# Weight parts of later mixers, made during the feed-forward before and kept in DRAM

## The chip, the core and the metric

The kernel runs on one core of one Trainium2 chip, in one launch. The metric is the device time of the launch in microseconds; the number shown for a kernel is the median of its runs. TensorE (PE) multiplies, VectorE (DVE), ScalarE (ACT) and GpSimd (POOL) do the element-wise work, and SyncE (SP) issues nearly all DMAs. All arithmetic that counts here is in float32.

## The reference

Four layers run one after another on one sequence of 512 tokens with 1024 channels: two layers of a first kind, then two of a second. Each layer is a mixer and a feed-forward:

```
first kind                                     second kind
h = rms_norm(x);  z = h @ w_in      (2560)     h = rms_norm(x);  p = h @ w_in_2    (10032)
attention, HGRN2 both ways, convolution        NSA, stick-breaking, GLA, forgetting attention
x = x + concat(mixers) @ w_out                 x = x + (sum of gate_n * (y_n @ w_branch_n)) @ w_out_2
x = x + square(relu(rms_norm(x) @ w1)) @ w2    x = x + square(relu(rms_norm(x) @ w1)) @ w2
```

The feed-forward is 1024 to 4096 to 1024 in all four layers.

## The kernel before

**Products of split operands.** A float32 product is made of three matmuls on a rounded type. Each operand is split into a high part (a rounded copy, by ACT) and a low part (the operand minus the high part, by DVE); `mm3` adds high·high, low·high and high·low in one PSUM bank. The activations (`xh`, `xl`) are split once a layer. A weight is split where it is used: `wload` (L321) takes a weight in units of 128 partitions x 512 floats (256 KB), loads each into a tile `wr` by a DMA on SP (L330), copies it to `wh` and writes the rest to `wl`. There are 4 `wr`, 4 `wh` and 3 `wl` tiles. A unit is four 128x128 blocks and 12 matmuls of 512 columns, or, in `nlater`, two blocks of 256 columns and 24 matmuls of 256 columns.

**Who splits.** `split` (L312) uses ACT (L315) and DVE (L316). In the mixers of the first kind, a counter (`share`, `pool_share`) lets the first 8 units go that way, and all later ones give the subtraction to POOL instead (L334 ACT, L335 POOL):

```
self.share += self.pool_share
if self.share >= 1.0:
    self.share -= 1.0
    nc.scalar.activation(hi, raw, AF.Copy)
    nc.gpsimd.tensor_tensor(lo, raw, hi.bitcast(F32), op=ALU.subtract)
else:
    self.split(hi, lo, raw)
```

**The order of the work.** Mixers are Python generators that `weave` runs by written-out times; projections that a mixer needs later are `Later` objects in a queue, and each step of a mixer advances the queue by a set rate (`pace`, `step`). Nothing of it is decided on the chip: the program is one fixed list of instructions for each engine, with semaphores between them, and a scheduler that the program asks for puts that list together. In a layer of the first kind the two HGRN heads, the convolution and the attention are woven, and then the attention's rest with half of the output projection. In the second kind NSA comes first, with its own projections (`nsa_inputs`, `compress`) and those of the queue beside it, then stick-breaking, GLA and the forgetting attention. `compress` loads other weights as they are into the same four `wr` tiles (L1477) and multiplies them unsplit (L1482).

**The feed-forward.** `mlp` (L496) goes in four chunks of 1024 hidden channels: 8 products with `w1` (ACT relu, POOL square, split into `hid`), then 8 products with `w2` (DVE times `R2`, POOL adds to `x`). That makes 64 products of two units each. In the last chunk `post(m)` makes the next layer's `xh`, `xl` and sums of squares.

Of the kernel before, what the change touches and what calls it, by code (L numbers as in the profile page):

```python
# [19 lines left out]
F32 = mybir.dt.float32  # L20
F32R = mybir.dt.float32r
# [8 lines left out]
T = 512  # L30
D = 1024
KT = D // 128
# [129 lines left out]
class Core:  # L162
    def __init__(self, ctx, tc, const):
        self.tc, self.nc = tc, tc.nc
        nc = self.nc
# [21 lines left out]
        self.keep = tc.dram_tile([KT, 128, T], F32, name="keep")  # L187
        self.pad(self.core_w, 96)
# [132 lines left out]

    def wload(self, pieces, a, b):

        nc = self.nc
        out, n = [], 512 // b
        for i in range(0, a, n):
            m = min(n, a - i)
            raw, hi, lo = self.wtile("wr", m, b), self.wtile("wh", m, b, F32R), self.wtile("wl", m, b, F32R)
            for ap, rows, cols in pieces:
                nc.sync.dma_start(raw[rows, :, cols], ap[:, i:i + m])  # L330
            self.share += self.pool_share
            if self.share >= 1.0:
                self.share -= 1.0
# [4 lines that stand above are left out]
            out += [(hi[:, k], lo[:, k]) for k in range(m)]  # L338
        return out

    def wcols(self, w, k0=0, kt=KT):

        v = w[k0 * 128:(k0 + kt) * 128, :].rearrange("(k p) c -> p k c", p=128)
        return self.wload([(v, slice(None), slice(None))], kt, v.shape[2])
# [155 lines left out]
    def mlp(self, w1, w2, post, tags, fc=1024):  # L500

        nc = self.nc
        nfc, nk = w1.shape[1] // fc, fc // 128
        R2 = self.t(tags["r2"], "R2")
        for c in range(nfc):
            hs = []
            for m in range(nk):
                col = c * fc + m * 128
                pz = self.tproj(w1[:, col:col + 128])
                r, s = self.t(tags["r"], "r"), self.t(tags["s"], "s")  # L510
                nc.scalar.activation(r, pz, AF.Relu)  # L511
                nc.gpsimd.tensor_tensor(s, r, r, op=ALU.mult)  # L512
                a, b = (self.t(tag, "hid", F32R) for tag in tags["h"][m])
                self.split(a, b, s)
                hs.append((a, b))
                if c == 0 and m == 1:
                    nc.vector.tensor_tensor(R2, self.R, self.R, op=ALU.mult)
            for m in range(KT):
# [4 lines left out]
                (nc.vector if last and m == KT - 1 else nc.gpsimd).tensor_tensor(self.x[m], self.x[m], s, op=ALU.add)  # L523
                if last:
                    post(m)

# [294 lines left out]
class First:  # L821
# [219 lines left out]

    def hgrn(self, l, pr, vi, slot, mix):
# [6 lines left out]
        for half in range(2):  # L1049
            h = 2 * pr + half  # L1050
            wv = lambda c: w[:, c:c + 64].rearrange("(k p) c -> p k c", p=128)
            ws = K.wload([(wv(1280 + h * 64), slice(None), slice(0, 64)),
                              (wv(1536 + h * 64), slice(None), slice(64, 128))], KT, 128)
# [194 lines left out]
    def layer(self, l, gmlp, post):  # L1248
# [17 lines left out]
        K.out_proj(w[0:512], [K.parts(y, "h", "hx") for y in at], lambda m: K.prep(m, gmlp()))  # L1266
        K.mlp(I["w_mlp_in"][l], I["w_mlp_out"][l], post,
# [12 lines left out]
class Second:  # L1280
# [120 lines left out]


    def narrow(self, l, other):
        K, nc, I = self.K, self.K.nc, self.I
        w = I["w_in_2"][l]
        ws = K.wload([(w[:, c:c + 32].rearrange("(k p) c -> p k c", p=128), slice(None), slice(32 * i, 32 * i + 32))
                          for i, c in enumerate((O_NG, O_FF, O_GA, O_GA))], KT, 128)
# [609 lines left out]
    def layer(self, l, gff, post):  # L2017
# [31 lines left out]
                   lambda m: K.prep(m, gff()), kept=True)  # L2049
        K.mlp(I["w_ff1_2"][l], I["w_ff2_2"][l], post,  # L2050
# [60 lines left out]
```

## Time and profile before

| | us |
|---|---|
| median of three runs | 3739.27 |
| lowest and highest run | 3739.17, 3741.41 |
| the profiled execution | 3740.83 |
| its span (first to last instruction) | 3738.3 |
| mean granted clock of TensorE | 0.989 |

The profile is of one execution, so what is summed from it is summed against 3740.83. Of the span, the feed-forwards take 347 to 697, 1012 to 1382, 2178 to 2528 and 3370 to the end (the second and the last with a piece of what stands around them); the mixers lie between, the first from 0. "Busy" of PE needs care: a 512-column matmul is drawn as some 390 ns, but in a feed-forward 1550 matmuls fill 350 us, one each 226 ns, so short waits of PE hide under the drawn ends.

### The profile page before, as it was taken

The numbers are of one execution on the slowest core, as the hardware profiler recorded it, in microseconds if no ns is written. First come the engines' busy times: TensorE is split into PE (matmuls) and PEld (weight loads), VectorE is DVE, ScalarE is ACT, GpSimd is POOL, SyncE is SP. The second block draws the span as 40 slices with busy tenths as digits, with TensorE's granted clock in tenths as the row PEclk, the third lists the DMA queues.
The fourth block names the chain that finished last, engine by engine and source line by source line (L and its number), as shares of the span: only waits on it lengthen the run. The fifth ranks groups of instructions, "written<-read, shape, count | busy, mean of one in ns | idle before, by whom it ended". The sixth has DMA issues, their size and how long they took to land.

```text
span 3738.3 us, 53178 instructions
## 1 busy us (share of the span) xinstructions
PE 3620.1 (97%) x18793; PEld 3010.6 (81%) x18793; DVE 2316.7 (62%) x4554; ACT 1900.7 (51%) x3940; POOL 947.6 (25%) x925
## 2 busy tenths in 40 slices
PE   8889999987999999999999999999999999999999
PEld 7757888885788887888788888887888888788887
DVE  8885333699543346787778753335687777874334
ACT  6575333467643343678554643334567744553333
POOL 4732222466122230001213122222001121222222
PEclk9999999999999999999999999999999999999999
DMA  4102333321133344213222243334312223233332
GB/s 130 52 12 77 96 98 96 113 60 29 43 96 96 98 117 128 55 46 75 65 72 68 74 114 97 97 98 128 93 32 71 71 65 77 60 105 95 97 97 87
DMA packets 561851, 306.65 MB, mean 82 GB/s; under 512 B 49978, under 2 KB 551344, under 8 KB 561584
## 3 DMA queue, kind: packets, MB, share of 16 engines
q1 hardware_dynamic: 558128, 296.95, 28.8%
q10 hardware_dynamic: 3456, 6.29, 0.4%
q8 instruction: 148, 2.42, 0.3%
q14 instruction: 119, 0.97, 0.1%
HBM read 292.68 MB, written 10.49 MB: 81 GB/s over the span
## 4 chain that ended last, share of the span: by engine, by line
PE 84%; DVE 11%; ACT 2%; issue 1%; DMA 1%; POOL 1%; SPq 0%; POOLq 0%; DVEq 0%; ACTq 0%
PE pm L348 21%; PE pm L350 21%; PE pm L349 21%; PE po L645 2%; PE pm L395 2%; PE pm L394 2%; PE pm L396 2%; DVE cy L1207 1%; PE pt L627 1%; PE pa L1022 1%; DVE X L1114 1%; DVE X L1115 1%; DVE acc L1136 1%; DVE nm L592 1%; PE pt L1959 1%
## 5 line engine op out<-in xcount | busy, mean ns | idle before, releaser
L316 DVE TENSOR_TENSOR wl<-wr,wh 128x512 fp32r<-128x512 f32 x956 | 677.9, 709 | 753.3 <-issue 383.2
L315 ACT ACTIVATE wh<-wr 128x512 fp32r<-128x512 f32 x956 | 600.8, 629 | 1039.8 <-PE pm L349 899.7
L348 PE MATMUL pm<-xh,wh 128*128 128x512 f32 x2160 | 855.0, 396 | 6.8 <-DVE zq L1048 2.8
L350 PE MATMUL pm<-xh,wl 128*128 128x512 f32 x2160 | 850.4, 394 | 7.8 <-POOL wl L335 7.8
L349 PE MATMUL pm<-xl,wh 128*128 128x512 f32 x2160 | 846.9, 393 | 0.0
L350 PEld LDWEIGHTS pm<-xh,wl 128*128 128x128 f32 x2160 | 407.1, 188 | 94.7 <-POOL wl L335 10.9
L348 PEld LDWEIGHTS pm<-xh,wh 128*128 128x128 f32 x2160 | 407.5, 189 | 89.4 <-DVE z L560 3.5
L349 PEld LDWEIGHTS pm<-xl,wh 128*128 128x128 f32 x2160 | 407.6, 189 | 82.6 <-issue 2.8
L350 PE MATMUL pm<-hid,wl 128*128 128x512 f32 x1024 | 398.1, 389 | 0.0
L349 PE MATMUL pm<-hid,wh 128*128 128x512 f32 x1024 | 398.0, 389 | 0.0
L348 PE MATMUL pm<-hid,wh 128*128 128x512 f32 x1024 | 396.5, 389 | 0.0
L523 POOL TENSOR_TENSOR x<-x,os 128x512 f32<-128x512 f32 x124 | 206.2, 1663 | 421.8 <-DVE os L521 420.1
L512 POOL TENSOR_TENSOR s<-r 128x512 f32<-128x512 f32 x128 | 135.0, 1055 | 572.2 <-ACT r L511 533.1
L394 PE MATMUL pm<-wh,xh 128*128 128x256 f32 x896 | 257.8, 291 | 5.5 <-ACT wh L315 3.9
L395 PE MATMUL pm<-wl,xh 128*128 128x256 f32 x896 | 258.0, 289 | 2.3 <-DVE wl L316 2.1
L396 PE MATMUL pm<-wh,xl 128*128 128x256 f32 x896 | 256.3, 287 | 0.0
L349 PEld LDWEIGHTS pm<-hid,wh 128*128 128x128 f32 x1024 | 192.2, 188 | 40.1
L350 PEld LDWEIGHTS pm<-hid,wl 128*128 128x128 f32 x1024 | 192.2, 188 | 39.9
L348 PEld LDWEIGHTS pm<-hid,wh 128*128 128x128 f32 x1024 | 192.2, 188 | 39.7
L348 PE MATMUL pm<-mxh,wh 128*128 128x512 f32 x512 | 202.3, 398 | 8.3 <-ACT mxh L315 5.3
L521 DVE TENSOR_TENSOR os<-pm,R 128x512 f32<-128x512 f32 x128 | 88.5, 692 | 191.5 <-PE pm L350 191.5
L349 PE MATMUL pm<-mxl,wh 128*128 128x512 f32 x512 | 202.8, 396 | 0.9 <-DVE mxl L316 0.9
(619 smaller groups left out, 6753.3 us busy)
## 6 DMA issues: line engine op xcount, KB each, us to landing
wr<-in_w_in_dram SPq DMA_DIRECT2D x376, 256.0 KB
wr<-in_w_ff_dram SPq DMA_DIRECT2D x256, 256.0 KB
wr<-in_w_mlp_in_dram SPq DMA_DIRECT2D x128, 256.0 KB
wr<-in_w_mlp_out_dram SPq DMA_DIRECT2D x128, 256.0 KB
wr<-in_w_out_dram SPq DMA_DIRECT2D x64, 256.0 KB
wr<-in_w_branch_dram SPq DMA_DIRECT2D x64, 256.0 KB
xo<-keep SPq DMA_DIRECT2D x32, 256.0 KB
keep<-x ACTq DMA_DIRECT2D x24, 256.0 KB
```

What stands on the lines that cost most here:

```text
L315: nc.scalar.activation(hi, src, AF.Copy)
L316: nc.vector.tensor_tensor(lo, src, (hi if hi_in is None else hi_in).bitcast(F32), op=ALU.subtract)
L348: nc.tensor.matmul(out, wh, xh, start=start, stop=False)
L349: nc.tensor.matmul(out, wh, xl, start=False, stop=False)
L350: nc.tensor.matmul(out, wl, xh, start=False, stop=stop)
L394: nc.tensor.matmul(o, self.xh[kk][:, c], h, start=f, stop=False, skip_group_check=True)
L395: nc.tensor.matmul(o, self.xh[kk][:, c], l, start=False, stop=False, skip_group_check=True)
L396: nc.tensor.matmul(o, self.xl[kk][:, c], h, start=False, stop=e, skip_group_check=True)
L512: nc.gpsimd.tensor_tensor(s, r, r, op=ALU.mult)
L521: nc.vector.tensor_tensor(s, po, R2, op=ALU.mult)
L523: (nc.vector if last and m == KT - 1 else nc.gpsimd).tensor_tensor(self.x[m], self.x[m], s, op=ALU.add)
L645: nc.tensor.matmul(*x, start=start and n == 0, stop=stop and n == len(mm) - 1, skip_group_check=True)
```

## The change

During each of the first three feed-forwards the kernel also splits weights of the mixer that follows. `split_ahead` makes a list of jobs, one for each unit: a load of the unit into a tile (`c` in the first kind, `g` in the second) on SP's queue; at the next step ACT's copy and DVE's subtraction into two more tiles; at the step after that two stores of 256 KB, issued on ACT's queue, into a DRAM tile. `background` is called after each of the 64 products and starts jobs at an even rate. `wload` asks for each unit whether it was kept; if so, it loads both parts straight into `wh` and `wl` by two DMAs on SP and neither takes a `wr` tile nor splits, and the counter of `pool_share` isn't moved.

Kept are 48 units for layer two (all of `w_in`, and rows 512 to 1024 of `w_out`), and 62 units each for layers three and four (the first gate's eight column blocks, the narrow columns, NSA's keys, values and queries, and stick-breaking's inputs). Layer one, GLA, the forgetting attention, the branches and the rest of the output projections load and split as before.

```diff
+    def units(self, pieces, a, b):
+        n = 512 // b
+        return [([(ap[:, i:i + min(n, a - i)], rows, cols) for ap, rows, cols in pieces], min(n, a - i))
+                for i in range(0, a, n)]
...
+    def split_ahead(self, tags, wanted, steps):
+        nc, todo = self.nc, [(u, m, b) for w in wanted for u, m in self.units(*w) for b in (w[2],)]
+        def job(unit, m, b):
+            view = lambda t: t[:, :m * b].rearrange("p (a b) -> p a b", a=m)
+            raw = view(self.t(tags[0], "pr"))
+            for ap, rows, cols in unit:
+                nc.sync.dma_start(raw[rows, :, cols], ap)
+            yield
+            hi, lo = (self.t(tag, "pp", F32R) for tag in tags[1:])
+            self.split(view(hi), view(lo), raw)
+            yield
+            d = self.tc.dram_tile([2, 128, T], F32, name="parts")
+            for i, x in enumerate((hi, lo)):
+                nc.scalar.dma_start(d[i][:, :m * b], x[:, :m * b].bitcast(F32))
+            self.kept[self.unit_key(unit)] = d
+        self.jobs, self.running = [job(*t) for t in todo], []
+        self.job_rate, self.job_credit = len(todo) / steps, 0.0
+
+    def background(self, last=False):
+        if not self.jobs and not getattr(self, "running", None):
+            return
+        self.job_credit += self.job_rate
+        while self.running or (self.jobs and last):
+            self.running = [j for j in self.running if next(j, self) is not self]
+            if not last:
+                break
+        while self.jobs and self.job_credit >= 0.5:
+            self.job_credit -= 1
+            j = self.jobs.pop(0)
+            next(j)
+            self.running.append(j)
...
     def wload(self, pieces, a, b):
-        out, n = [], 512 // b
-        for i in range(0, a, n):
-            m = min(n, a - i)
-            raw, hi, lo = self.wtile("wr", m, b), self.wtile("wh", m, b, F32R), self.wtile("wl", m, b, F32R)
-            for ap, rows, cols in pieces:
-                nc.sync.dma_start(raw[rows, :, cols], ap[:, i:i + m])
+        out = []
+        for unit, m in self.units(pieces, a, b):
+            hi, lo = self.wtile("wh", m, b, F32R), self.wtile("wl", m, b, F32R)
+            d = self.kept.pop(self.unit_key(unit), None)
+            if d is not None:
+                for i, x in enumerate((hi, lo)):
+                    nc.sync.dma_start(x.bitcast(F32), d[i][:, :m * b].rearrange("p (a b) -> p a b", a=m))
+                out += [(hi[:, k], lo[:, k]) for k in range(m)]
+                continue
+            raw = self.wtile("wr", m, b)
+            for ap, rows, cols in unit:
+                nc.sync.dma_start(raw[rows, :, cols], ap)
             self.share += self.pool_share
...
     def mlp(self, w1, w2, post, tags, fc=1024):
                 self.split(a, b, s)
                 hs.append((a, b))
+                self.background()
...
                 (nc.vector if last and m == KT - 1 else nc.gpsimd).tensor_tensor(self.x[m], self.x[m], s, op=ALU.add)
+                self.background()
                 if last:
                     post(m)
+        self.background(last=True)
...
     First.layer
+        nxt = self.ahead(1) if l == 0 else Second.ahead(K, I, 0)
+        K.split_ahead(("c", "hz", "hx"), nxt, 64)
         K.mlp(I["w_mlp_in"][l], I["w_mlp_out"][l], post,
...
     Second.layer
+        K.split_ahead(("g", "z", "k"), self.ahead(K, I, 1) if l == 0 else [], 64)
         K.mlp(I["w_ff1_2"][l], I["w_ff2_2"][l], post,
```

`First.ahead` and `Second.ahead` list the units in about the order in which the mixers take them; `both_ways` and `narrow_columns` give two loads that gather columns a name, so that both places ask for the same unit.

## Rows read from the trace of the kernel before

**Rows 1.** The page, part 1: busy time, share of span, instructions by engine.

```profile
...
PE 3620.1 (97%) x18793; PEld 3010.6 (81%) x18793; DVE 2316.7 (62%) x4554; ACT 1900.7 (51%) x3940; POOL 947.6 (25%) x925
...
```

**Rows 2.** Windows by stage: us, PE, PEld, DVE, ACT, POOL, clock, DMA, GB/s.

```profile
...
697.00:1012.00 315.00, 280.20 (x1571) 222.12 (x1570) 251.43 (x417) 202.69 (x415) 159.87 (x162) 0.96 0.17 48
1382.00:2178.00 796.00, 781.59 (x4527) 664.21 (x4526) 609.44 (x1445) 473.98 (x1090) 122.46 (x154) 1.00 0.29 76
2178.00:2528.00 350.00, 350.00 (x1551) 289.66 (x1550) 139.38 (x208) 123.83 (x211) 85.82 (x68) 1.00 0.35 102
...
```

**Rows 3.** Windows inside mixers two, three and four; columns as in rows 2.

```profile
...
760.00:935.00 175.00, 148.58 (x863) 120.47 (x862) 162.20 (x257) 115.02 (x234) 116.11 (x113) 0.94 0.14 40
1390.00:1490.00 100.00, 93.67 (x558) 76.46 (x557) 68.32 (x259) 37.50 (x78) 7.73 (x26) 0.98 0.47 131
1490.00:1650.00 160.00, 158.61 (x1132) 140.52 (x1131) 129.11 (x383) 109.87 (x320) 2.44 (x4) 1.00 0.18 46
2550.00:2650.00 100.00, 94.29 (x568) 76.89 (x568) 53.25 (x146) 38.55 (x79) 8.24 (x20) 1.00 0.44 121
...
```

**Rows 4.** Chain of waits by line: 760:935, 1390:1490, 2550:2650.

```profile
...
by line: DVE cy L1207 13.8%; DVE acc L1136 5.3%; DVE X L1114 5.2%; DVE X L796 5.1%; DVE X L806 4.8%; issue 4.3%; DVE X L1115 4.2%; DVE X L795 4.1%; DVE nm L592 3.9%; PE ps L1126 3.9%; DVE rot L934 2.9%; DVE qs L669 2.4%; PE pm L394 2.0%; PE
...
by line: DVE cb L1463 8.3%; PE pm L395 8.1%; PE pm L394 7.8%; PE pm L396 7.5%; DMA wr<-in_w_in_dram 6.0%; DMA wr<-in_nsa_cmp_wv_dram 5.3%; DVE wl L316 5.1%; PE pm L348 5.1%; PE pm L350 5.0%; PE pm L349 5.0%; SPq L217 4.9%; PE ps L1482 4.6%;
...
by line: PE pm L348 14.2%; PE pm L350 13.8%; PE pm L349 13.7%; DMA wr<-in_nsa_cmp_wv_dram 8.7%; PE pm L395 7.2%; PE pm L394 6.7%; PE pm L396 6.5%; SPq L1477 6.3%; DMA wr<-in_w_in_dram 5.7%; PE ps L1482 4.8%; DVE wl L316 2.0%; issue 1.5%; AC
...
```

**Rows 5.** Groups by form, VectorE, 697:1012: busy us, mean ns | idle before.

```profile
...
L1207 DVE SCALAR_TENSOR_TENSOR cy<-u,cw,cy 128x512 f32<-128x512 f32 x30 | 33.7, 1124 | 0.3
...
L1114 DVE TENSOR_TENSOR X<-X,x 128x256 f32<-128x256 f32 x18 | 13.7, 763 | 0.7 <-ACT X L807 0.7
L796 DVE TENSOR_TENSOR X<-z,m 128x256 f32<-128x256 f32 x12 | 11.1, 925 | 0.0
...
L316 DVE TENSOR_TENSOR wl<-wr,wh 128x512 fp32r<-128x512 f32 x9 | 6.2, 690 | 8.4 <-issue 6.4 <-PE pm L350 1.2 <-ACT xh L445 0.9
...
```

**Rows 6.** Lines 1207, 1114, 796 in 697:1012: duration ns minimum/median/maximum.

```profile
...
L1207 DVE SCALAR_TENSOR_TENSOR cy<-u,cw,cy x30: 731/878/1848, 792.7 to 908.5; 128x512 f32<-128x512 f32 x30
...
L1114 DVE TENSOR_TENSOR X<-X,x x18: 408/425/1516, 749.9 to 956.7; 128x256 f32<-128x256 f32 x18
...
L796 DVE TENSOR_TENSOR X<-z,m x12: 411/726/1539, 731.1 to 930.4; 128x256 f32<-128x256 f32 x12
...
```

**Rows 7.** Timeline from 915: start us, us, engine, line, operation.

```profile
...
915.08 1.46 POOL L1205 TENSOR_TENSOR cy<-cy,tap 128x512 f32<-128x512 f32 x1 [0.90 <-ACT tap L1204]
...
915.32 1.49 DVE L796 TENSOR_TENSOR X<-z,m 128x256 f32<-128x256 f32 x1
...
917.67 0.41 DVE L796 TENSOR_TENSOR X<-x 128x256 f32<-128x256 f32 x1
...
```

**Rows 8.** Groups by form of GpSimd, 697 to 1012; columns as in rows 5.

```profile
...
L335 POOL TENSOR_TENSOR wl<-wr,wh 128x512 fp32r<-128x512 f32 x39 | 57.2, 1470 | 28.9 <-PE pm L396 10.5 <-PE pm L350 7.1 <-ACT wh L334 4.3
...
```

**Rows 9.** Pieces of the chain, 1390 to 1490: start us, us, what.

```profile
...
1452.51 3.06 DMA wr<-in_w_in_dram
1455.59 0.64 ACT wh L315
1456.26 0.69 DVE wl L316
...
```

**Rows 10.** DMA issues on SyncE's and ScalarE's queues: duration ns minimum/median/maximum.

```profile
...
L330 SPq DMA_DIRECT2D wr<-in_w_mlp_in_dram x16: 367/368/368, 428.2 to 468.4; - x16
...
L1477 SPq DMA_DIRECT2D wr<-in_nsa_cmp_wk_dram x16: 595/601/622, 1420.1 to 1464.4; - x16
...
L450 ACTq DMA_DIRECT2D keep<-x x5: 326/326/327, 1360.2 to 1378.3; - x5
...
```

**Rows 11.** Groups by form of TensorE, 1390 to 1490; columns as in rows 5.

```profile
...
L394 PE MATMUL pm<-wh,xh 128*128 128x256 f32 x96 | 27.4, 295 | 2.2 <-ACT wh L315 2.2
L348 PE MATMUL pm<-xh,wh 128*128 128x512 f32 x54 | 21.6, 401 | 1.4 <-DVE z L560 1.4
...
```

More of the change, by code (lines that the diff above doesn't have):

```diff
@@ L187, in __init__ @@
         self.keep = tc.dram_tile([KT, 128, T], F32, name="keep")
+        self.kept, self.jobs = {}, []
         self.pad(self.core_w, 96)
@@ L320, in wtile, with unit_key @@
         return self.core_w.tile([128, n], dt, name=tag, tag=tag, bufs=WEIGHTS[tag])[:, :a * b].rearrange("p (a b) -> p a b", a=a)
+    def units(self, pieces, a, b):
+        n = 512 // b
+        return [([(ap[:, i:i + min(n, a - i)], rows, cols) for ap, rows, cols in pieces], min(n, a - i))
+                for i in range(0, a, n)]
+    @staticmethod
+    def unit_key(unit):
+        return tuple((ap.tensor.name, ap.offset, str(ap.ap), str(cols)) for ap, rows, cols in unit)
+    def split_ahead(self, tags, wanted, steps):
[15 more added lines that the diff above has]
+        self.job_rate, self.job_credit = len(todo) / steps, 0.0
@@ L339, in wload, with wrows, wanted @@
         return out
+    @staticmethod
+    def wrows(w, k0=0, kt=KT):
+        v = w[k0 * 128:(k0 + kt) * 128, :].rearrange("(k p) c -> p k c", p=128)
+        return [(v, slice(None), slice(None))], kt, v.shape[2]
     def wcols(self, w, k0=0, kt=KT):
-        v = w[k0 * 128:(k0 + kt) * 128, :].rearrange("(k p) c -> p k c", p=128)
-        return self.wload([(v, slice(None), slice(None))], kt, v.shape[2])
+        return self.wload(*self.wrows(w, k0, kt))
+    def wanted(self, w, *cols):
+        out = []
+        for c, n in cols:
+            per = 512 // n
+            out += [self.wrows(w[:, c:c + n], i, per) for i in range(0, w.shape[0] // 128, per)]
+        return out
     def mm3(self, out, wh, wl, xh, xl, start, stop):
@@ L1039, in att_out, with both_ways, ahead @@
         return y
+    @staticmethod
+    def both_ways(w, h):
+        wv = lambda c: w[:, c:c + 64].rearrange("(k p) c -> p k c", p=128)
+        return [(wv(1280 + h * 64), slice(None), slice(0, 64)), (wv(1536 + h * 64), slice(None), slice(64, 128))], KT, 128
+    def ahead(self, l):
+        K, w, o = self.K, self.I["w_in"][l], self.I["w_out"][l]
+        out = K.wanted(w, (768, 128)) + [self.both_ways(w, 0)] + K.wanted(w, (896, 128)) + [self.both_ways(w, 2)]
+        out += K.wanted(w, (2304, 128), (512, 256), (2048, 128), (1024, 256)) + [self.both_ways(w, 1), self.both_ways(w, 3)]
+        out += K.wanted(w, (2432, 128), (0, 256), (2176, 128), (256, 256), (1792, 128), (1920, 128))
+        return out + K.wanted(o[512:1024], *((m * 128, 128) for m in range(KT)))
     def hgrn(self, l, pr, vi, slot, mix):
@@ L1050, in hgrn @@
             h = 2 * pr + half
-            wv = lambda c: w[:, c:c + 64].rearrange("(k p) c -> p k c", p=128)
-            ws = K.wload([(wv(1280 + h * 64), slice(None), slice(0, 64)),
-                              (wv(1536 + h * 64), slice(None), slice(64, 128))], KT, 128)
+            ws = K.wload(*self.both_ways(w, h))
             pz = K.pt()
@@ L1400, in rope, with ahead, narrow_columns @@
         nc.vector.tensor_tensor(v[:, :, 0:16], v[:, :, 0:16], b, op=ALU.add)
+    @staticmethod
+    def ahead(K, I, l):
+        w = I["w_in_2"][l]
+        out = K.wanted(w, (O_GATE, 128)) + [Second.narrow_columns(w)]
+        out += K.wanted(w, (O_KC, 128), (O_VC, 128), (O_KS, 256), (O_KS + 256, 256), (O_Q, 256), (O_Q + 256, 256))
+        out += K.wanted(w, *((O_GATE + m * 128, 128) for m in range(1, KT)))
+        out += K.wanted(w, (O_SB + 1024, 256), (O_SB, 128), (O_SB + 512, 128), (O_SB + 128, 128), (O_SB + 640, 128))
+        return out + K.wanted(w, (O_SB + 1280, 256), *((O_SB + c, 128) for c in (256, 768, 384, 896)))
+    @staticmethod
+    def narrow_columns(w):
+        return [(w[:, c:c + 32].rearrange("(k p) c -> p k c", p=128), slice(None), slice(32 * i, 32 * i + 32))
+                for i, c in enumerate((O_NG, O_FF, O_GA, O_GA))], KT, 128
     def narrow(self, l, other):
@@ L1405, in narrow @@
         w = I["w_in_2"][l]
-        ws = K.wload([(w[:, c:c + 32].rearrange("(k p) c -> p k c", p=128), slice(None), slice(32 * i, 32 * i + 32))
-                          for i, c in enumerate((O_NG, O_FF, O_GA, O_GA))], KT, 128)
+        ws = K.wload(*self.narrow_columns(w))
         p = K.pt()
```

## The prediction

> **What bounds the kernel now.** I read the page first. PE is drawn busy 97% of the span, the other engines far less [rows 1], so a gain must come out of PE's waits, and only 118 us of idle time is drawn. Then the windows by stage. The feed-forwards have none of it: 350.00 of 350.00 us, and DVE and ACT are at 139 and 124 us there. Layer two's mixer is the loose one: PE has 280.2 of 315 us, 34.8 idle, at a granted clock of 0.96; layer three's has 14.4 idle in 796 us [rows 2]. Inside layer two, from 760 to 935, PE idles 26.4 of 175 us while DVE is busy 162.2 [rows 3], and the chain of waits runs through DVE lines (1207, 1136, 1114, 796, 806), hardly through products of weights [rows 4]. DVE sets the pace of that stretch.
>
> Layers three and four are loose at their start, where NSA's projections run: 6.3 and 5.7 us of PE are idle in 100 [rows 3]. There the chain does go through weights. In a window of 100 us a percent is a microsecond: 6.0 us of raw loads and 5.1 us of subtractions `wl` in layer three, 5.7 and 2.0 in layer four [rows 4]. One round of it: a load of 3.06 us, then ACT's copy of 0.64, then DVE's 0.69 [rows 9]; the four `wr` tiles are shared with `compress`, so the load starts late. After that, in 1490 to 1650, PE is idle 1.4 us [rows 3].
>
> **The change, part by part.**
>
> *Layer two.* All 40 units of `w_in` and 8 of `w_out` come as parts. Two things leave DVE's stretch. First, the eight subtractions that DVE makes itself, 8 x 0.69 = 5.5 us [rows 5]. Second, GpSimd's: 57.2 of its 159.9 busy us [rows 8, 2]. These count because GpSimd's work slows DVE's. An L796 of 128x256 that starts 0.24 us after a GpSimd instruction of 1.46 us takes 1.49 us; two microseconds later, with GpSimd still, one takes 0.41 [rows 7]. Over the stage three groups show it best, by their mean against their minimum [rows 5, 6]: L1207 30 x (1.124 - 0.731) = 11.8 us, L1114 18 x (0.763 - 0.408) = 6.4, L796 12 x (0.925 - 0.411) = 6.2, together 24.4. The weight subtraction is 57.2/159.9 = 0.36 of GpSimd's time, so 8.7 us of that is its own: the floor, for these groups are only 58.5 of DVE's 251.4 busy us. The ceiling is that each of them holds DVE for its whole length, 57.2, but no more than PE's idle 34.8 can come out. I take twice the floor, 18, since the one pair shown is a nearly full hold and other DVE groups lose too. With 5.5 it is 23.5 us of DVE; before 760 and after 935 DVE isn't always last, so I count 22, with ends of 8 and 34.8. ACT's 48 copies go too, but ACT has 202.7 of 315 us and isn't what is waited for.
>
> The Trainium skill bears on the pair (SBUF — State Buffer, section "Who interferes with whom"): VectorE and GpSimd share one pair of ports as an exclusive lock, and a VectorE instruction with two SBUF inputs waits for the whole of a GpSimd instruction that reads SBUF. By that rule alone the sum takes the ceiling in place of 18; the trace agrees for the pair, 1.49 against 0.41 us, and only in part for the sum, where the median L1114 is at its minimum. The rival "all of it" is what this rule gives.
>
> *Layers three and four, the dense start.* A kept unit needs no `wr` tile, no copy and no subtraction. Of layer three's chain 5.1 us of `wl` and some 3 of `wh` (pieces of 0.64) are gone. Of the 6.0 of raw loads none, some or all come back as waits for the parts: the trace shows no load into `wh` or `wl`. Its cost is bounded by nothing (landed before PE asks) and by its landing. Two issues of 0.37 us [rows 10] and a landing as in rows 9 make 3.4 to 3.8 us from the moment a tile is free. It may be filled once PE has left the unit three before, so two units of PE's work cover it: a unit takes 12 x 0.226 = 2.7 us, from 1550 matmuls in 350 us [rows 2], so 5.4 us. That covers it by the nearest row, so I count 9 us in layer three, ends 0 and 14. In layer four 2.0 of `wl`, about as much of `wh`, and a part of 5.7: 6, ends 0 and 9.
>
> *The rest of NSA and stick-breaking.* 62 subtractions are 43 us of DVE's 609 in a mixer [rows 2]. From 1490 DVE has 129 of 160 us but PE hardly idles, so little is to be had: 3 us a layer for what hides under PE's drawn ends, ends 0 and 8.
>
> *The feed-forwards.* A job adds 0.64 + 2 x 0.33 = 1.3 us to ACT (the stores' issues are on its queue [rows 10]) and 0.69 to DVE. For 62 jobs that is 80 and 43 us on top of 124 and 139, in 350 [rows 2]: both stay under 60%. On SP it is 62 x 0.37 = 23 us among loads that are four `wr` tiles ahead. In bytes it is 62 x 0.77 MB = 48 MB in 350 us, 137 GB/s on top of 102. At the stage's own price (0.35 for 102) the DMA share would go to 0.82; the highest share of the rows shown is 0.47 [rows 3], so this is the part that I know least. What covers it is that every load is wanted several units later. The stores' wait for DVE's subtraction stands on ACT's queue a whole product (5.4 us) after it, with the next relu and weight copies behind it. I count nothing in the loop, and at each of three ends a copy and a subtraction that stand ahead of the last `post(m)`, 1.3 at most: 2 us in all. If the cover fails, 172 jobs pay.
>
> *SP's queue.* The part loads stand in line with all else on it. In layer three the constants' issues take 4.9 us of the chain [rows 4], and a kept unit behind them has only 5.4 us of cover where a raw unit had four `wr` tiles and three `wl`: 2 us, ends 0 and 5.
>
> The sum: -22 - 9 - 6 - 6 + 2 + 2 = -39 us, so 3740.8 - 39 = 3701.8 for the profiled execution. The median of the runs is 1.6 us below that execution, so **3700**.
>
> **The rivals.**
>
> *All of it.* GpSimd's hold costs DVE its full length and PE's whole idle time of layer two goes (34.8), the weights' chain in layers three and four too (14 and 9), 6 for the rest, less 4: -60, 3679. For it: DVE at 93% in the stretch, and the full hold in rows 7. Against: with DVE shorter, the HGRN levels' own chain through PE and ACT stands there. Chance 0.15.
>
> *Little of it.* What GpSimd still does (102.7 us, its convolution adds above all) closes up and holds DVE instead, so layer two gives its 5.5 and a little, 8; the loads of parts take the place of the raw loads, 8 and 3; with 2 and 4: 3741 - 8 - 8 - 3 - 2 + 4 = 3724, so 3722. For it: line 1205's adds are as long as the subtractions (1.46 against 1.47 us, rows 7, 8). Chance 0.17.
>
> *Given back.* The jobs delay the feed-forwards' own splits or loads. At 0.2 us for each of 172 jobs that is 34 us, 3734 for the runs; or the names of the units don't match and the mixers load and split as before, 3743. Against the first: PE doesn't wait once in 350 us. Chance 0.07.
>
> *Slower: three buffers are too few.* The load of a `wl` tile waits for PE, with SP's later loads behind it. If parts land later than 5.4 us after release, PE waits in each dense unit. In the 100 us of layer three there are 96/8 + 54/4 = 25.5 such units [rows 11], in both layers 51. At 6.7 us it is 1.3 x 51 = 66 us; the gains there are gone and layer two's 22 stay: 3741 - 22 + 66 + 4 = 3789, so 3787. From about 5.8 us on, layer two's gain is eaten. For it: `compress` puts four issues of 0.6 us [rows 10] between the parts, 2.4 us, and two loads take the place of one. Against: 3.4 to 3.8 us without them. Chance 0.11.
>
> The Trainium skill (DMA: Bandwidth & Descriptors, section "Latency and other measured facts") speaks for this rival: access to HBM is 0.2 us on average and 2 us at high load. With 1.8 us more, an estimate from that page, the parts would land 5.2 to 5.6 us after release, at the edge of the cover. No run here shows such a load yet; at a share of 0.47 the landing is 3.06 us.
>
> **How the numbers follow.** The forecast holds 0.50, with a range of its own from 3687 to 3714, by the ends of layer two's term. Faster by over 0.2% (7.5 us, about what can be told here) takes the forecast and the first two rivals, 0.80 of their 0.82; slower takes 0.12; the rest, 0.08, is the same. From 3672 to 3735 the forecast, both other faster cases and half of "given back" lie; outside are the slower case and the tails, some 0.19.
>
> **What would show it.** In the profile after: no L335 left in layer two's mixer, L1207's and L1114's means there near their minima, DVE's busy time lower by about 23 us and the stage shorter by about as much. In 1390 to 1490 no `wr` of `w_in`, no `wl` on DVE; if PE now waits for DMA into `wh` or `wl`, the slow rival has begun. The three feed-forwards at the same length within 1 us, DMA share 0.6 to 0.8. I would be wrong if a feed-forward grows by over 3 us, if layer two's mixer gains under 8 us, or if waits for the parts sum to over 20 us.

## The result, and the profile after

The changed kernel takes 3774.39 us (median of 4 runs, 3769.68 to 3776.63); the kernel before, on the same chip, 3740.34 (4 runs). The ratio is 1.0087, with an interval from 1.0074 to 1.0099. The change makes the kernel 34 us slower, where 39 us faster was forecast. The profiled execution of after took 3772.6 us, its span 3770.8.

Where did the time go? Both kernels have the same 18793 matmuls, so their progress can be compared: when PE starts its n-th matmul in each. This table is worked out from the two traces. The first column is a time in the span of before, the others say how many microseconds later (+) or earlier the changed kernel stands at the same count, and how much of that came since the mark above. Inside a mixer the scheduler puts some matmuls in another order, so there the n-th is not always the same one; the marks are read to a tenth or two.

```
mark in before        what lies above the mark              after stands    since the mark above
 697                  mixer one, feed-forward one           +13.7           +13.7
1012                  layer two's mixer                      -2.4           -16.1
1382                  feed-forward two                      +17.7           +20.1
1490                  layer three's dense start             +10.2            -7.5
2080                  rest of layer three's mixer           +17.9            +7.7
2528                  its output, feed-forward three        +41.8           +23.9
2650                  layer four's dense start              +36.4            -5.5
end                   rest of layer four                    +33.0            -3.4
```

The mixers do give time back, 16.1 us in layer two and 7.5 and 5.5 at the two dense starts. The feed-forwards, at which the prediction counted 2 us in all, take 57.7.

Of before, the windows over feed-forwards one and two (as in [rows 2]: us, then PE, PEld, DVE, ACT, POOL, clock, DMA share, GB/s); the third is in [rows 2]:

```profile
347.00:697.00 350.00, 350.00 (x1550) 289.63 (x1549) 137.78 (x210) 125.62 (x215) 93.75 (x69) 1.00 0.35 102
1012.00:1382.00 370.00, 370.00 (x1640) 306.22 (x1639) 150.49 (x230) 135.35 (x229) 97.39 (x72) 1.00 0.35 101
```

And of after: the same three feed-forwards, then layer two's mixer and layer three's dense start:

```profile
348.00:711.00 363.00, 355.97 (x1552) 289.67 (x1551) 179.06 (x256) 147.79 (x255) 94.88 (x71) 1.00 0.60 189
1010.00:1400.00 390.00, 377.78 (x1640) 306.15 (x1639) 206.39 (x291) 166.54 (x287) 95.80 (x72) 0.99 0.68 216
2199.00:2570.00 371.00, 359.32 (x1554) 290.49 (x1553) 186.75 (x264) 154.39 (x265) 87.13 (x69) 0.99 0.64 205
...
711.00:1010.00 299.00, 276.90 (x1571) 219.56 (x1570) 215.20 (x409) 179.67 (x371) 104.17 (x123) 0.97 0.32 99
...
1407.70:1500.20 92.50, 90.05 (x558) 74.12 (x557) 52.06 (x234) 21.52 (x51) 6.87 (x26) 1.00 0.70 212
```

1640 matmuls that filled 370 us take 390, and PE idles 12.2 of them. Yet DVE has only 206 of the 390 us, ACT 167, the DMA engines 0.68: no engine is near its end. That speaks against the amount of work and for the place where it stands; the experiments below test it. The page's 40 slices (94 us each; DMA busy tenths, then GB/s) show how unevenly it stands:

```profile
DMA  4106933541498346323232399335622223233332
GB/s 130 51 12 205 338 118 96 159 130 42 123 338 295 95 133 203 107 79 76 65 74 62 83 347 341 104 97 168 186 68 82 73 62 76 66 100 99 98 98 87
```

The traffic that the prediction had evenly at 0.82 over a feed-forward is at 0.8 to 0.9 and 295 to 347 GB/s in its first half (slices 5, 12 and 13, 24 and 25), and falls back to 95 to 118, about what before has, in the slice after (6, 14, 26). The instructions of the jobs' part tiles say the same (number, duration in ns minimum/median/maximum, first and last start in us):

```profile
L349 ACTq DMA_DIRECT2D parts<-pp x344: 325/327/1852, 302.1 to 2356.4; - x172
L316 ACT ACTIVATE pp<-pr x172: 610/624/645, 300.6 to 2346.5; 128x512 fp32r<-128x512 f32 x172
L317 DVE TENSOR_TENSOR pp<-pr,pp x172: 675/685/1802, 324.6 to 2355.6; 128x512 fp32r<-128x512 f32 x172
its engine sat idle before it (us, times) until:
  DMA pr<-in_w_in_dram: 49.0, 30
  ACT pp L316: 36.1, 33
  DVE pp L317: 23.3, 18
  DMA parts<-pp: 19.4, 9
```

The first copy is at 300.6 us, in mixer one, 47 us before the feed-forward in whose loop it is written, and the last of layer four's at 2346.5, where that feed-forward goes on to 2570. The scheduler has put the jobs into the engines' lists far ahead of where `background` stands in the program; that it goes as early as their tiles allow is my reading. And in an engine's list nothing overtakes: while ACT waits for a job's load (49.0 us in all), everything behind stands still. One such place in feed-forward two, from the timeline of after (start, duration, engine; in brackets the idle time before, and what ended it):

```profile
1052.25 0.63 ACT L316 ACTIVATE pp<-pr 128x512 fp32r<-128x512 f32 x1 [0.82 <-DMA pr<-in_w_in_dram]
1052.29 2.77 SPq L342 DMA_DIRECT2D pr<-in_w_in_dram  x3
1052.31 4.16 ACTq L349 DMA_DIRECT2D parts<-pp  x3
...
1056.57 0.63 ACT L316 ACTIVATE wh<-wr 128x512 fp32r<-128x512 f32 x1 [3.69 <-DMA parts<-pp]
...
1057.23 1.49 DVE L317 TENSOR_TENSOR wl<-wr,wh 128x512 fp32r<-128x512 f32 x2 [3.03 <-ACT wh L316]
...
1058.86 0.60 ACT L577 ACTIVATE r<-pm 128x512 f32<-128x512 f32 x1 [0.87 <-DVE wl L317]
...
1059.51 0.79 PE L414 MATMUL pm<-xh,wh 128*128 128x512 f32 x1 [4.29 <-ACT r L577]
```

Three stores hold ACT's queue for 4.16 us. The third is issued only at 1056.14: its queue waits for a semaphore whose last update comes at 1056.07, from the landing of a store issued at 1050.49. Behind the stores stands a weight's copy, behind it DVE's `wl`, then the relu that empties the PSUM bank, and PE stands 4.29 us, its longest wait in that feed-forward. It is a wait for an eviction that has nothing to do with any job.

### The profile page after: what moved, and what is told of

It reads as the page before. It is cut to its first block, busy times and chain, and to the rows that moved or that the text cites. A ratio compares the mean times of both kernels' runs of the same rounds, so it can differ in the third digit from the quotient of the medians.

```text
span 3770.8 us, 54180 instructions
## 1 busy us (share of the span) xinstructions
PE 3629.7 (96%) x18793; PEld 2999.2 (80%) x18793; DVE 2352.8 (62%) x4594; ACT 1895.0 (50%) x3940; POOL 888.7 (24%) x885
## 4 chain that ended last, share of the span: by engine, by line
PE 76%; DVE 6%; DMA 6%; ACT 2%; issue 1%; POOL 0%; ACTq 0%; SPq 0%; DVEq 0%; POOLq 0%
PE pm L414 19%; PE pm L416 19%; PE pm L415 19%; PE pm L460 2%; PE pm L461 2%; PE pm L462 2%; DMA pr<-in_w_in_dram 2%; DMA parts<-pp 2%; PE po L714 2%; PE pt L696 1%; DVE pp L317 1%; DVE wl L317 1%; DMA wr<-in_w_mlp_out_dram 1%; DVE nm L661 1%; PE pa L1091 1%
## 5 line engine op out<-in xcount | busy, mean ns | idle before, releaser
L317 DVE TENSOR_TENSOR wl<-wr,wh 128x512 fp32r<-128x512 f32 x824 | 605.2, 736 | 577.5 <-issue 266.9
L316 ACT ACTIVATE wh<-wr 128x512 fp32r<-128x512 f32 x824 | 515.3, 628 | 759.0 <-PE pm L415 648.9
L416 PEld LDWEIGHTS pm<-hid,wl 128*128 128x128 f32 x1024 | 192.2, 188 | 52.0 <-DVE wl L317 12.5
L416 PE MATMUL pm<-mxh,wl 128*128 128x512 f32 x512 | 203.2, 397 | 0.7 <-DVE wl L317 0.7
```

Of the source, the lines that this page charges most:

```text
L316: nc.scalar.activation(hi, src, AF.Copy)
L317: nc.vector.tensor_tensor(lo, src, (hi if hi_in is None else hi_in).bitcast(F32), op=ALU.subtract)
L416: nc.tensor.matmul(out, wl, xh, start=False, stop=stop)
```

## The experiments

All were compared with the kernel before on the same chips; its medians there were 3741.05, 3739.96 and 3740.77 us for the three groups of runs below.

**First group: which part of a job costs?**

*e1_paced.* Each job's load keeps its place in SP's list:

```
-                nc.sync.dma_start(raw[rows, :, cols], ap)
+                self.tc.keep_in_program_order(nc.sync.dma_start(raw[rows, :, cols], ap))
```

> The changed kernel, and each job's load is pinned behind the SyncE load that stands before it in the program, so that jobs run at the written rate (one in 1.0 to 1.3 products) instead of in the first 150 us of a feed-forward. Crowding theory (it doesn't matter whether through DMA or through the engines' lists): the 58 us that the three feed-forwards and the projections before them lost fall under 10, DMA share there under 0.75, time 3715 to 3730. Amount theory (172 jobs cost what they cost, wherever they stand): the loss stays above 40, time 3758 to 3775.

Measured: 3753.5 us, ratio 1.0036 [1.0023, 1.0048], so 21 us better than the changed kernel, and in neither of the two ranges. By the progress of PE feed-forward one now costs 1.0 us in place of 13.7, all of it ahead of the loop; the other two still cost 19.8 and 20.4. That is not spread either: between marks 12 us apart it comes in four steps of 3.7 to 5.8 us in each of the two, one at the turn from the first to the second half of each chunk, and almost nothing in between. The first of them, from the timeline:

```profile
1080.07 0.63 ACT L316 ACTIVATE pp<-pr 128x512 fp32r<-128x512 f32 x1 [2.64 <-DMA pr<-in_w_in_dram]
...
1080.73 0.69 DVE L317 TENSOR_TENSOR pp<-pr,pp 128x512 fp32r<-128x512 f32 x1 [3.03 <-ACT pp L316]
...
1081.94 0.68 DVE L588 TENSOR_TENSOR os<-pm,R 128x512 f32<-128x512 f32 x1
...
1082.77 0.47 PE L414 MATMUL pm<-hid,wh 128*128 128x512 f32 x1 [1.82 <-DVE os L588]
```

ACT waits 2.64 us for a job's load, DVE 3.03 for ACT's copy, and the eviction `os` stands behind both until PE has no free bank.

*e2_no_split.* Jobs load and store, but don't split; the raw tile is stored twice, so the parts are not the weight's parts and the products come out otherwise:

```
...
-            self.split(view(hi), view(lo), raw)
...
-                nc.scalar.dma_start(d[i][:, :m * b], x[:, :m * b].bitcast(F32))
+                nc.scalar.dma_start(d[i][:, :m * b], raw.rearrange("p a b -> p (a b)"))
```

> The changed kernel without the jobs' copy and subtraction: the raw unit is loaded and stored twice, so DMA traffic of the jobs is whole and ACT and DVE have only the two store issues a job; the mixers' products use wrong parts. DMA theory (loads of the feed-forward's own weights land late among the jobs' bytes): loss in the feed-forwards stays at 45 or more of 58, time 3760 to 3780. Lists theory (copies and subtractions that wait for their loads stand ahead of the feed-forward's own on ACT and DVE): loss under 15, time 3720 to 3735.

*e3_no_traffic.* The first job of a layer runs whole; all others split one resident tile of ones and neither load nor store, and all kept units load the first one's parts (the same remark on the products):

```
+            if first:
+                self.kept[self.unit_key(unit)] = first["d"]
+                yield
+                raw = first["raw"]
+                hi, lo = (self.t(tag, "pp", F32R) for tag in tags[1:])
+                self.split(hi, lo, raw)
+                yield
+                return
...
```

> The changed kernel with only one unit a layer loaded and stored; every further job makes its copy and its subtraction from a tile that lies there, with no load and no store, and all kept units in the mixers load that one pair of parts (products wrong). DMA theory: the feed-forwards lose under 10 of 58, time 3715 to 3728. Lists theory: they lose 40 or more, time 3755 to 3770.

*e4_one_job.* One whole job a layer, the others do nothing; the mixers load as many parts as in the changed kernel (the first job's). It is the mixers' side alone:

```
+            if first:
+                self.kept[self.unit_key(unit)] = first["d"]
+                return
...
```

> The mixers' side alone: one job a layer, and every kept unit loads that one pair of parts (products wrong). All theories: the feed-forwards last as before. By the trace of the changed kernel the mixers gain some 24 to 34 us, so 3706 to 3716; the forecast's own sum for the mixers was 43, which would be 3697.

Measured: e2 3743.26 us, ratio 1.0011 [1.0002, 1.0021]; e3 3747.83, 1.0023 [1.0013, 1.0032]; e4 3712.17, 0.9924 [0.991, 0.9937]. e4 lies in its range, e2 and e3 in none of theirs. The mixers' side is worth 29 us, the jobs cost 62 (3774.4 - 3712.2). Of these the traffic alone makes 31, the splits alone 36: both cost, and the two nearly add up, so neither the bytes nor the engines' time is the cause by itself. What they share is their place, which the second group tests. In e2 the loss is uneven: 26.9 us in feed-forward three, 2.0 in feed-forward two with as many jobs. Before the copies of weights ACT waits longer in the former for stores to land (its waits from 2140 to 2560, then from 990 to 1370: us, times, longest); why the two differ is open.

```profile
ACT wh L316 <- DMA parts<-pr: 40.0, 7, 8.0
...
ACT wh L316 <- DMA parts<-pr: 16.8, 5, 4.8
```

In e3, where the splits wait for no load, the copies written in layer three's feed-forward run from 2150 to 2222 us, before and at the start of the feed-forward: the progress of PE loses 13.4 us from 2080 to the mark at 2178 and 4.9 after it, and DVE has 100.4 of the 120 us from 2080 to 2200. Over all three layers:

```profile
L316 ACT ACTIVATE pp<-pr x172: 612/625/644, 303.7 to 2222.4; 128x512 fp32r<-128x512 f32 x172
L317 DVE TENSOR_TENSOR pp<-pr,pp x172: 674/678/1789, 326.2 to 2228.3; 128x512 fp32r<-128x512 f32 x172
```

**Second group: too early, too late, or too many?**

*e5_lead.* As e1, and one more product between load and split (`yield` twice, and 60 in place of 64 steps, so that the last job ends in time):

```
+                self.tc.keep_in_program_order(nc.sync.dma_start(raw[rows, :, cols], ap))
             yield
+            yield
...
```

> Change: the jobs' loads keep their place in SP's list as in e1_paced, and one more product passes between a job's load and its split (62 jobs are begun over 60 products, so that the last ones end with the feed-forward). Theory A (a late split holds up the lists): what e1_paced still lost, 20 us in each of the two feed-forwards with 62 jobs, is ScalarE and VectorE standing at a split whose load was issued only one product before, behind loads that wait for a buffer; evictions and the hidden tiles' splits queue behind it. With one more product of lead the steps of 4 to 5 us at the turns between the two halves go: 3712 to 3718 us, as with the mixers' side alone (3712.2). Theory B (too many jobs): 62 jobs in 64 products are more than the lists and the DMA engines take in whatever order: 3745 to 3755 us, as e1_paced (3753.5).

Measured: 3762.08 us, ratio 1.0066 [1.0051, 1.008]. Theory A's time is refuted, it is slower than e1; whether more lead helps it doesn't show, for the lead written into the program never reached the lists. The reason is in the idle times before the jobs' split; ahead of each copy stands its load, in nearly every job:

```profile
its engine sat idle before it (us, times) until:
  ACT pp L316: 425.9, 165
  DMA pr<-in_w_in_dram: 359.2, 161
```

The scheduler moved the copies back up to their loads; a `yield` in the program doesn't bind them. In layer three's feed-forward a copy starts 3.28 us after the issue of the last load before it (median), with 3.25 in e1. So loads that are spaced out make ACT wait 161 times (158 times and 326.2 us in e1), where the hoisted ones made it wait 30 times. Whether that stalls PE depends on what stands behind it.

*e6_lead_all.* As e5, with copy, subtraction and stores in program order too:

```
-            self.split(view(hi), view(lo), raw)
+            keep = self.tc.keep_in_program_order
+            keep(nc.scalar.activation(view(hi), raw, AF.Copy))
+            keep(nc.vector.tensor_tensor(view(lo), raw, view(hi).bitcast(F32), op=ALU.subtract))
...
-                nc.scalar.dma_start(d[i][:, :m * b], x[:, :m * b].bitcast(F32))
+                keep(nc.scalar.dma_start(d[i][:, :m * b], x[:, :m * b].bitcast(F32)))
```

> Change: as e5_lead, and the jobs' copies on ScalarE, subtractions on VectorE and stores keep their place in program order too, not the loads alone. If the order of the loads settles it (theory A as in e5_lead), this is as e5_lead within 4 us. If the splits and stores are also moved ahead by the scheduler and cost there, it is 5 to 30 us faster than e5_lead. Theory B: 3745 us or more.

Measured: 3711.05 us, ratio 0.9924 [0.9911, 0.9937]: 51 us below e5 (5 to 30 were expected of this case), 63 below the changed kernel, 29 below the kernel before, and as fast as e4, in which the jobs do nothing. The windows of its three feed-forwards:

```profile
348.50:698.50 350.00, 350.00 (x1550) 289.63 (x1550) 192.01 (x259) 154.34 (x262) 93.93 (x69) 1.00 0.68 209
994.00:1364.00 370.00, 370.00 (x1640) 306.31 (x1639) 217.30 (x291) 171.82 (x291) 97.14 (x72) 1.00 0.77 232
2155.00:2505.00 350.00, 350.00 (x1551) 289.76 (x1550) 199.43 (x266) 158.69 (x269) 85.07 (x67) 1.00 0.74 233
```

350.00, 370.00 and 350.00 us of PE, to the hundredth as before, with the copies of all but 3 of the 172 jobs in them, DVE 54 to 67 us busier, and the DMA engines at up to 0.77. This is also the answer to theory B: 62 jobs in 64 products are not too many.

*e7_fewer.* As e5, but layers three and four keep only the 24 units of the dense start; the later projections are split as before:

```
-        out += K.wanted(w, *((O_GATE + m * 128, 128) for m in range(1, KT)))
-        out += K.wanted(w, (O_SB + 1024, 256), (O_SB, 128), (O_SB + 512, 128), ...)
-        return out + K.wanted(w, (O_SB + 1280, 256), *((O_SB + c, 128) for c in (256, 768, 384, 896)))
+        return out
```

> Change: as e5_lead, but layers three and four keep only the 24 units of their dense start (gate, narrow columns, compressed and selected keys and values, queries); the 38 of the later projections are loaded and split as before. The mixers' side alone lost 4 us at the end of each of layer two's and layer four's sparse-attention stretches, where no unit fewer to split gave anything back. Theory A: as e5_lead, less those 8 us: 3704 to 3712 us. Theory B (too many jobs): 24 jobs fit, 3705 to 3715 us, some 35 us below e5_lead. If the late units do pay for themselves: 5 us or more above e5_lead.

Measured: 3724.5 us, ratio 0.9959 [0.9947, 0.9971]. With the splits left free, 24 jobs cost nothing in a feed-forward where 62 cost over 20 us, as theory B had it; but by e6, 62 can be free as well. The mixers give 12.5 us less than in e6 (17.8 against 30.3 from the mark at 697 on), so the time is above those that were forecast. 5.8 of these lie in layer three's stretch from 1800 to 2080, and not because raw units are split again there: e11 below splits them too and loses nothing in it (-0.7). PE's list for this stretch is that of before in all kernels but three, the changed one, e3 and e7 (the last two share one), and just these lose 3.6, 4.0 and 5.4 us in it; the others lie between -1.6 and +1.3. That the order is the cause was not tried. The loss in the stretch of sparse attention (below; where the forecast says layer two, layer three is meant) is here as well, 4.5 us in layer three and 4.6 in layer four, though spread over it, so the late units alone don't explain it.

*e8_splits_in_place.* e3 with the copies and subtractions in program order, as in e6 (the parts are one unit's, as in e3).

```
...
-                self.split(hi, lo, raw)
+                keep = self.tc.keep_in_program_order
+                keep(nc.scalar.activation(hi, raw, AF.Copy))
+                keep(nc.vector.tensor_tensor(lo, raw, hi.bitcast(F32), op=ALU.subtract))
```

> Change: as e3_no_traffic (jobs without load or store, one resident tile split 172 times), but the copies and subtractions keep their place in program order. Output is not the reference's: all kept units load one pair. Theory A: e3_no_traffic lost 36 us because the splits, which wait for nothing, were moved into the mixer ahead of the feed-forward, where VectorE is short; in their place under the 64 products they cost nothing: 3710 to 3716 us (mixers' side alone 3712.2). Theory B: the splits' time on the engines is what costs wherever they stand: 3740 to 3750 us, as e3_no_traffic (3747.8).

Measured: 3712.66 us, ratio 0.9926 [0.9913, 0.9939]. The same splits, 35 us less than e3, and nothing above e4. The copies now go on to 2535 us. PE's own list is no rival: against before it differs at 105 to 115 places in each feed-forward here, where nothing is lost, and at 25 in feed-forward two of e1, where 19.8 us are.

**Third group: is order enough, and whose?**

*e9_in_order.* The changed kernel with all instructions of the jobs in program order: e6 without the second `yield` and with 64 steps. 

> Change: as the changed kernel, with one product between a job's load and its split and 64 products to spread over, but the jobs' loads, copies, subtractions and stores all keep their place in program order (e6_lead_all without the extra product of lead). Theory C (the place of the splits and stores in the engines' lists is the whole loss): 3709 to 3716 us, as e6_lead_all (3711.1). Theory D (order and lead are both needed): a load issued one product ahead lands 3.3 us after its issue (median with paced loads), of a product's 5.45 us, and stands behind loads that wait for a buffer, so some splits are late: 3718 to 3745 us.

*e10_loads_free.* The same, but the loads are left to the scheduler as in the changed kernel:

```
-                self.tc.keep_in_program_order(nc.sync.dma_start(raw[rows, :, cols], ap))
+                nc.sync.dma_start(raw[rows, :, cols], ap)
```

> Change: as the changed kernel, but the jobs' copies, subtractions and stores keep their place in program order; the loads are left to the scheduler. Theory C: the loads can then only run ahead as far as the raw tiles allow, which the splits in their place set free one by one: 3709 to 3718 us. Rival E (loads moved ahead are what costs, by SP's list and the DMA engines): 3740 to 3775 us, near the changed kernel (3774.4).

*e11_layer_two.* e6 with jobs for layer two alone.

```
-        nxt = self.ahead(1) if l == 0 else Second.ahead(K, I, 0)
+        nxt = self.ahead(1) if l == 0 else []
-        K.split_ahead(("g", "z", "k"), self.ahead(K, I, 1) if l == 0 else [], 60)
+        K.split_ahead(("g", "z", "k"), [], 60)
```

> Change: as e6_lead_all, but parts are kept for layer two alone (48 units); layers three and four load and split as in the kernel before. By the progress of PE in e6_lead_all layer two gives 20 us less 1.5 lost before it, layers three and four some 5 each after the 4 that each loses at the end of sparse attention: 3719 to 3724 us. If the loss of 4 us is there whatever is kept: 3724 to 3730 us. If layers three and four gave nothing net: 3709 to 3714 us.

Measured: e9 3712.18 us, 0.9927 [0.9914, 0.9939]; e10 3712.79, 0.9924 [0.9911, 0.9938]; e11 3715.86, 0.9929 [0.9915, 0.9942]. Theory C holds and rivals D and E fall: neither the lead nor the loads' order is needed once copy, subtraction and stores stay in place. e11 lies in none of its three ranges. The idle times before the splits of e9 show why the shorter lead is enough; ACT waits for a load three times in 172:

```profile
L346 ACT ACTIVATE pp<-pr x172: 614/632/636, 369.7 to 2539.5; 128x512 fp32r<-128x512 f32 x172
L347 DVE TENSOR_TENSOR pp<-pr,pp x172: 674/684/1778, 371.4 to 2540.2; 128x512 fp32r<-128x512 f32 x172
its engine sat idle before it (us, times) until:
  DVE pp L347: 95.9, 61
  ACT hid L316: 17.0, 65
  DMA wr<-in_w_mlp_in_dram: 4.5, 4
  DMA pr<-in_w_in_dram: 4.1, 3
```

In e10 the loads can't run far ahead, because a raw tile comes free only with a split in its place: among SP's DMAs the first of the jobs' loads stands at place 95 there and in the changed kernel, at 114 in e9, but the 11th and 21st at 142 and 177 as in e9, with 123 and 140 in the changed kernel. e11 is 5 us slower than e6 by the medians, but the intervals overlap: layer two holds some 25 of 29 us of the gain, and what layers three and four add can't be told from nothing.

The last fence also shows what isn't the price: in e9 ACT idles 95.9 us, 61 times, before the jobs' copies, until the subtraction of another job ends (91.1 us in e6), more than the 49.0 that the changed kernel waits there for loads, and PE loses nothing. So ACT's idle time isn't the price by itself; what stands behind the wait, as in the timelines above, seems to be.

What each kernel lost in the three feed-forwards proper, by the progress of PE (us, from 347 to 697, 1012 to 1382 and 2178 to 2528 of before):

```
kernel                                  one    two   three
changed kernel                         12.8   20.0   20.4
e1, loads bound                         0.0   19.8   20.4
e2, no splits                           0.0    2.0   26.9
e3, no traffic                          4.9    7.7    4.9
e5, loads bound, a product of lead      0.1   21.8   26.0
e7, as e5, 24 jobs in two and three     0.1    0.0    0.0
e4, one job                             0.0    0.0    0.0
e8, e3 with splits bound                0.0    0.0    0.0
e6, e9, e10, splits and stores bound    0.0    0.0    0.0
```

What was lost ahead of the loops is not in it: the changed kernel lost another 0.9 us before 347 and 3.7 from 2080 to 2178, e3 13.4 in the latter.

## Why the prediction was wrong, step by step

**The feed-forwards: the step that failed.** The prediction put it: "What covers it is that every load is wanted several units later ... I count nothing in the loop", 2 us with the ends of the loops. Measured: 57.7 us. The step took the jobs to stand where the program writes them, one to a product, and reckoned shares of 350 us from that. They stood wherever the scheduler put them: the first copies 26 to 48 us ahead of each feed-forward, the rest bunched in its first half, the stores among the weights' copies. Its reckonings of shares hold for jobs that are in place: e6, e9 and e10 run all 172 and lose 0.0 us, at a DMA share of up to 0.77 (0.82 was the estimate), with the stores on ACT's queue a product after the split. Nor was the sum of the work to blame, only its place: e3 and e8 split the same tiles as often, and differ by 35 us.

The rival "given back" had the mechanism ("the jobs delay the feed-forwards' own splits or loads"), at 0.2 us a job and a chance of 0.07. The price was 57.7 / 172 = 0.34 us a job, and 3734 became 3774. Its argument against itself, that PE doesn't wait once in 350 us, spoke of a list in which the jobs were not yet standing.

**Layer two's mixer.** Forecast -22; -16.1 in after, and -18.2 to -20.0 in e4, e6 and e8 to e11, where the jobs of layer three split nothing before the mixer's end (in e4 and e8 one unit at most). The mechanism was right in sum and not in its parts. (In the pair of [rows 7] the slow instruction reads `z` and `m`, the fast one `x` alone; it is the group's minimum of 411 ns in [rows 6] that bears the reading out.) DVE's work fell by 36 us (251.4 in [rows 2], 215.2 after), more than the 23.5 reckoned. The three groups of after that answer to [rows 5]:

```profile
L1287 DVE SCALAR_TENSOR_TENSOR cy<-u,cw,cy 128x512 f32<-128x512 f32 x30 | 35.6, 1185 | 0.4
...
L1194 DVE TENSOR_TENSOR X<-X,x 128x256 f32<-128x256 f32 x18 | 9.7, 540 | 0.8 <-ACT X L876 0.8
...
L865 DVE TENSOR_TENSOR X<-z,m 128x256 f32<-128x256 f32 x12 | 5.3, 438 | 0.0
```

L796 (now L865) came down near its minimum of 411 ns, 925 to 438, and L1114 (L1194) from 763 to 540, so 9.9 us for the two. The largest, L1207 (L1287), didn't move: 1124 to 1185. GpSimd's other work of that stretch, the convolution's adds (L1285, 28 of 1432 ns), is as it was (28 of 1424 ns before), and it is the convolution's own DVE line that is still long. That is what the rival "little of it" had said, true of this line alone. PE's idle time in the stage is 299.0 - 276.9 = 22.1 us in after: DVE is 36 us shorter and the stage 16. In the chain of waits from 767 to 930, the stretch of [rows 4], the convolution's line still leads, 12.2% against 13.8%, while the rest is spread over many lines, and the chain through PE and ACT that the rival "all of it" had against it doesn't stand out:

```profile
by line: DVE cy L1287 12.2%; PE ps L1206 6.7%; PE pm L461 5.2%; PE pm L460 5.1%; issue 5.0%; PE pm L462 5.0%; DVE X L1194 4.2%; DVE nm L661 4.2%; POOL qn L1004 3.9%; DVE X L864 2.6%; DVE X L1195 2.5%; DVE acc L1216 2.5%; PE pa L1091 2.4%; P
```

The exclusive lock of the Trainium skill (SBUF — State Buffer, section "Who interferes with whom") lets DVE gain GpSimd's 57.2 us at the most, if each subtraction holds a DVE instruction for its whole length. With its own eight subtractions (5.5) DVE gained 36.2, so 30.7 at most of them: more than the 18 taken here, and about half of that ceiling.

**The dense starts.** Forecast -9 and -6; measured -7.5 and -5.5 in after, -7.1 and -4.9 in e6. The rival of three buffers, 0.11, is refuted: in the whole execution one wait of PE's matmuls for the load of a part is drawn, the row from the waits of after:

```profile
PE pm L461 <- DMA wl<-parts: 0.4, 1, 0.4
```

though the DMA share at layer three's dense start is 0.70. From issue to landing the loads of `wl` took 2.87 us (median of all 172, by the semaphores in the trace), 3.8 at the 90th percentile; at layer three's dense start 3.3 and 4.2, inside the 5.4 of cover.

**The rest of NSA and stick-breaking.** Forecast -3 a layer; by e6's progress +2.3 us in layer three and -0.6 in layer four. 43 us of DVE's work gone gave nothing; PE hardly waited there (1.4 us idle in 160 [rows 3]). Layer four's -0.6 is better than what the parts did: in 2990 to 3240 PE's list is in another order than before's in every kernel, and all gain 1.0 to 5.0 us there, e11, which keeps nothing for that layer, 4.9. In the stretch that ends with sparse attention (1490 to 1650, 2650 to 2810) each layer loses 4 to 6.5 us in every kernel that keeps parts for it, e4 too; e11, which keeps none there, gains 1.2 in each. In e4 one wait of PE is drawn at its end (waits of 1612 to 1632 us):

```profile
PE pt L702 <- DVE pe L1749: 2.3, 1, 2.3
```

PE's list is in another order there than before, in e4 at 971 places from 1490 to 1650. So is e11's, at 498, which loses nothing, so another order alone isn't enough; which order costs, and why, was not tried and stays open.

**SP's queue.** Forecast +2: no wait for it can be seen. **The sum** of e6's own terms is then 1.5 (ahead of the first job) - 20.0 - 7.1 + 2.3 - 4.9 - 0.6 = -28.8, with 0.0 for the feed-forwards, against -43 forecast for the mixers. The mixers' side gave two thirds of its forecast; the sign was lost in the feed-forwards.

## What to carry to other kernels

Here the work that was to hide in the gaps of a full stage cost by its place in the engines' lists, not by its share of their time: with a scheduler between program and lists, read from the lists where each piece will stand, or bind it. Binding the loads alone took back 21 of 63 us, since the consumer then waited at the head of its list; binding copy, subtraction and stores took back all. Which of these three it needs was not tried. If a stage has grown and no engine in it is near its end, look at the slices of the page for bunching, and at what an eviction that came late had in front of it.

## What the runs showed of the hardware that was not expected

Twice the traffic of before under a full PE cost nothing when its splits and stores were spread evenly: 232 GB/s in place of 101 at a DMA share of 0.77 in e6, with no wait of PE in 370 us. Bunched to over 300 GB/s and 0.9 of the engines, landing grew: in after the jobs' loads took 5.0 us from issue to landing (median, by the semaphores) against 3.3 in e1_paced and 3.5 in e6, and the 90th percentile of the feed-forward's own loads went from 2.9 to 3.0 us before to between 5.0 and 6.0 (4.3 to 4.8 in e6, where it cost nothing). The Trainium skill (DMA: Bandwidth & Descriptors, section "Latency and other measured facts") has 0.2 us for an access to HBM on average and 2 at high load; the 1.7 us between 3.3 and 5.0 are of that size, but no run here ties them to HBM, and they show only under the bunch: at layer three's dense start, at 0.70, `wl` parts landed in 3.3. A store's issue on ACT's queue takes 0.33 us, but up to 1.85 in after and 1.72 in e6.
